# Memory values of a decoder trunk as seven half-size products, woven with two query heads (one core, Trainium2)

## The chip, the cores and the metric

The kernel runs on one core of one Trainium2 chip. The metric is the device time of one execution in microseconds (us). The kernel before took 1379.85 us in the median of three runs (1379.85 to 1380.17).

## The reference

Two decoder layers over x of 512 rows and 1024 columns. Each layer has three sub-layers, each `x = x + RMSNorm_post(f(RMSNorm_pre(x)))`: a mixer (layer 0: forgetting attention beside a gated convolution; layer 1: a recurrent block), a cross-attention of four heads into 256 memory rows, and a SwiGLU feed-forward of width 2816. The change is in the cross-attention:

```python
def memory_cross_attention(h, m, w_q, w_kv, w_o):
    q = (h @ w_q).reshape(bsz, seq, MEM_HEADS, MEM_HEAD_DIM)      # 4 heads of 256
    k, v = jnp.split(m @ w_kv, 2, axis=-1)                        # m: 256 x 1024
    s = jnp.einsum("bqhd,bkhd->bhqk", q, k) * (MEM_HEAD_DIM ** -0.5)
    p = jax.nn.softmax(s, axis=-1)
    o = jnp.einsum("bhqk,bkhd->bqhd", p, v).reshape(bsz, seq, D_MODEL)
    return o @ w_o
```

with `h = RMSNorm_pre(x)` and `m = RMSNorm(mem) * g_mem`. So the values are V = m @ W_v, a 256 x 1024 by 1024 x 1024 product in each layer.

## The kernel before

**Number format.** Every operand of a product is split into a high and a low part (`wh` and `wl`, `hTh` and `hTl`, `vh` and `vl`): ScalarE (ACT) casts the high part, VectorE (DVE) subtracts it from the source to get the low part. A product is three matmuls on TensorE (PE): high by high, high by low, low by high. A matmul here takes a 128 x 128 stationary operand and streams 512 columns. Weights come in pieces of 128 x 1024 values (512 KB) through a pool of four staging buffers `st`, and are split into pools of four `wh` and four `wl` buffers (`load_w`; `split_out` for other operands, L553-L562). Such a buffer can be cast into again when the last matmul that reads its old content is done.

**Order.** PE runs its instructions in the order of the program text. On ACT, DVE and GpSimd (POOL) a scheduler sets the order when the kernel is built; the chip then runs each engine's list from front to back, and an instruction that waits holds up all behind it on its engine. SyncE (SP) issues the weight loads and GpSimd some transfers.

**The stages around the change**, in each layer:
- The mixer's output projection (`OutProj.half1`, L613) goes over four blocks t of 128 rows. After each, `chain` (L637) ends the block: the square of the bank on ACT (`junk<-bB`, L221), the mean on DVE (`post`, L225 and L229), its power -0.5 on POOL (L233), the gain (`yb`, L642), and the two halves of the residual sum (`x`, L645). When block t has run half of its matmuls, `next` (L653) normalises block t-1 for the cross-attention: squares of x on ACT, `pre` on DVE (L225, L229) and POOL (L233), and two halves `h` on DVE (L259). Block t-2 is transposed there: eight 128 x 128 transposes on PE (L306), then `hTh` on ACT (L315) and `hTl` on DVE (L316). The transposes of block t need both halves of `h`.
- `memory_T` (L1019) makes the memory, transposed and scaled by its gain, in high and low parts `mT` (L1043, L1044) from `mTr` (the normalised memory without the gain).
- `memory_kv` (L1057) makes the keys in four quarters, each with two weight pieces and two banks of 8 steps (a 512-column and a 256-column matmul, L1071 and L1072, per step); each bank ends in `ks` on ACT and DVE (L1074, L1075), each quarter in the split `kh`, `kl`. Then `rest` transposes the last two row blocks, and the values are made: for each half of the columns four weight pieces, each used by two banks of three matmuls per step (L1088 to L1090), 96 matmuls in all, and a split `vh`, `vl` per bank.
- `cross` (L1095) makes the four query heads (`q_head`, L1102, 48 matmuls each by way of `ws_steps`), scores, softmax and the attention outputs, the first two query heads right after the values.
- In the feed-forward, `DownProj` already works with seven half-size products; its sums of weights are made in DRAM by copies (the list `copies`, which `pace` hands to SP behind the weight loads) and by adds (the list `adds`, accumulating transfers of GpSimd, which `spend` hands out at set places).

## Time and profile before

| | |
|---|---|
| median of three runs | 1379.85 us (1379.85 to 1380.17) |
| the profiled execution | 1379.94 us, of which the span from the first to the last instruction is 1378.2 us |
| mean granted PE clock | 0.999 |
| busy share of the span | PE 99%, DVE 81%, ACT 53%, POOL 8% |
| moved by DMA | 233.34 MB |
| keys, layer 0 | from 227.08 us |
| values, layer 0 | from 251.35 us |

In a timeline a row gives the start (us from the span's start), the duration, the engine, the line, output and inputs by their names, how many instructions run on in the row, and in brackets how long the engine had idled before it and what ended that. In a group of instructions the row gives the count, the busy time with the mean of one in ns, and the idle time ahead of them. Lines are those of the kernel before.

### The profile page before, as it was taken

How to read it: one execution, taken by the hardware profiler on the slowest of the kernel's cores; microseconds unless marked ns; L12 is line 12 of the kernel's file. 1: busy time of each engine (PE TensorE's matmuls, PEld its weight loads, DVE VectorE, ACT ScalarE, POOL GpSimd, SP SyncE). 2: the span in 40 equal slices, each digit the busy share in tenths (PEclk: the TensorE clock that was granted, in tenths of full speed). 3: DMA queues.
4: the chain of work that ended last, by engine and by line, in shares of the span. 5: the costliest groups of instructions: out<-in, count | busy, mean ns of one | idle time of the engine just before them, and what ended most of it. 6: DMA issues, size and time to landing. Idle time of an engine off the chain costs nothing.

```text
span 1378.2 us, 21545 instructions
## 1 busy us (share of the span) xinstructions
PE 1368.9 (99%) x8262; PEld 1217.7 (88%) x8262; DVE 1119.8 (81%) x1850; ACT 730.9 (53%) x1206; POOL 111.2 (8%) x160
## 2 busy tenths in 40 slices
PE   9999999999999999999999999999999999999998
PEld 7888788888899999998889888888889999999886
DVE  6777778635589999989898898764568999999987
ACT  5345466534464444456684896553456444445664
POOL 1000001012000101000011000101200011000001
PEclk9999999999999999999999999999999999999999
DMA  6854353668125557566666657357712555666654
GB/s 222 287 174 162 109 194 88 206 154 169 62 92 167 150 148 187 161 246 217 201 221 189 217 170 246 84 185 156 155 61 93 169 155 171 157 176 237 201 190 144
DMA packets 155107, 233.34 MB, mean 169 GB/s; under 512 B 8462, under 2 KB 90482, under 8 KB 153724
## 3 DMA queue, kind: packets, MB, share of 16 engines
q1 hardware_dynamic: 134420, 179.73, 39.5%
q0 software_dynamic: 17072, 46.16, 15.2%
q10 hardware_dynamic: 3512, 6.08, 1.4%
q8 instruction: 65, 1.06, 0.3%
q14 instruction: 38, 0.31, 0.1%
HBM read 219.34 MB, written 58.74 MB: 202 GB/s over the span
## 4 chain that ended last, share of the span: by engine, by line
PE 99%; DVE 0%; DMA 0%; ACT 0%; issue 0%; DVEq 0%; SPq 0%; ACTq 0%
PE bA L337 13%; PE bA L339 13%; PE bA L338 13%; PE bB L337 6%; PE bB L338 6%; PE bB L339 6%; PE bB L822 3%; PE bB L823 3%; PE bB L821 3%; PE bA L1071 2%; PE bA L822 2%; PE bA L823 2%; PE bA L821 2%; PE bA L580 2%; PE bA L582 2%; PE bB L582 2%
## 5 line engine op out<-in xcount | busy, mean ns | idle before, releaser
L557 DVE TENSOR_TENSOR wl<-st,wh 128x1024 fp32r<-128x1024 f32 x108 | 131.2, 1220 | 83.9 <-ACT wh L556 83.3
L556 ACT CAST wh<-st 128x1024 fp32r<-128x1024 f32 x108 | 113.1, 1050 | 107.9 <-PE bA L338 55.1
L337 PE MATMUL bA<-hTh,wh 128*128 128x512 f32 (+1 forms) x440 | 168.6, 383 | 0.0
L339 PE MATMUL bA<-hTh,wl 128*128 128x512 f32 (+1 forms) x440 | 165.6, 376 | 0.0
L338 PE MATMUL bA<-hTl,wh 128*128 128x512 f32 (+1 forms) x440 | 165.5, 376 | 0.0
L448 ACT CAST wg<-wr 128x1024 fp32r<-128x1024 f32 x80 | 83.6, 1046 | 48.9 <-DVE wr L477 38.5
L787 ACT CAST wh<-st 128x1024 fp32r<-128x1024 f32 x76 | 74.9, 985 | 62.4 <-PE bA L823 27.0
L449 DVE TENSOR_TENSOR wg<-wr,wg 128x1024 fp32r<-128x1024 f32 x80 | 97.1, 1214 | 0.0
L337 PEld LDWEIGHTS bA<-hTh,wh 128*128 128x128 f32 x440 | 82.9, 188 | 15.3 <-issue 1.0
L339 PEld LDWEIGHTS bA<-hTh,wl 128*128 128x128 f32 x440 | 82.8, 188 | 15.3
L338 PEld LDWEIGHTS bA<-hTl,wh 128*128 128x128 f32 x440 | 83.0, 189 | 13.8
L792 DVE TENSOR_TENSOR wl<-st,wh 128x1024 fp32r<-128x1024 f32 x76 | 86.1, 1133 | 10.2 <-ACT wh L787 10.1
L448 ACT CAST wh<-tt 128x1024 fp32r<-128x1024 f32 x40 | 42.1, 1053 | 61.4 <-DVE tt L477 61.4
L337 PE MATMUL bA<-hTq,wh 128*128 128x256 f32 x208 | 59.2, 284 | 0.0
L339 PE MATMUL bA<-hTq,wl 128*128 128x256 f32 x208 | 58.9, 283 | 0.0
L338 PE MATMUL bA<-hTq,wh 128*128 128x256 f32 x208 | 58.8, 283 | 0.0
L821 PE MATMUL bB<-wh,ya 128*128 128x512 f32 x148 | 57.6, 389 | 0.0
L822 PE MATMUL bB<-wl,ya 128*128 128x512 f32 x148 | 57.6, 389 | 0.0
L823 PE MATMUL bB<-wh,ya 128*128 128x512 f32 x148 | 57.6, 389 | 0.0
L767 DVE TENSOR_TENSOR ya<-yb,ya 128x512 fp32r<-128x512 f32 x84 | 53.3, 638 | 0.0
L821 PE MATMUL bA<-wh,ya 128*128 128x512 f32 x132 | 51.3, 389 | 0.0
L822 PE MATMUL bA<-wl,ya 128*128 128x512 f32 x132 | 51.3, 389 | 0.0
(385 smaller groups left out, 4396.9 us busy)
## 6 DMA issues: line engine op xcount, KB each, us to landing
wr<-in_w_ffn_gu_dram SPq DMA_DIRECT2D x80, 512.0 KB
st<-t SPq DMA_DIRECT2D x40, 512.0 KB
t<-in_w_ffn_down_dram SPq DMA_DIRECT2D x32, 512.0 KB
st<-in_w_xkv_dram SPq DMA_DIRECT2D x32, 512.0 KB
st<-in_w_ffn_down_dram SPq DMA_DIRECT2D x30, 512.0 KB
st<-in_ab_w_in_dram SPq DMA_DIRECT2D x24, 512.0 KB
y<-yr POOLq DMA_DIRECT2D x18, 512.0 KB, 4.7
t<-in_w_ffn_down_dram POOLq DMA_DIRECT2D x16, 512.0 KB, 8.7
```

What stands on the lines that cost most here:

```text
L337: nc.tensor.matmul(out=ps, lhsT=wh, rhs=xh, start=first, stop=False)
L338: nc.tensor.matmul(out=ps, lhsT=wh, rhs=xl, start=False, stop=False)
L339: nc.tensor.matmul(out=ps, lhsT=wl, rhs=xh, start=False, stop=last)
L448: return (lambda: nc.scalar.copy(out=to[0], in_=src), lambda: nc.vector.tensor_tensor(out=to[1], in0=src, in1=f(to[0]), op=ALU.subtract))
L449: lambda: nc.vector.tensor_tensor(out=to[1], in0=src, in1=f(to[0]), op=ALU.subtract))
L556: nc.scalar.copy(out=hi, in_=src)
L557: nc.vector.tensor_tensor(out=lo, in0=src, in1=f(hi), op=ALU.subtract)
L787: nc.scalar.copy(out=self.wt[s][0], in_=self.st[s])
L792: nc.vector.tensor_tensor(out=lo, in0=self.st[s], in1=f(hi), op=ALU.subtract)
L821: nc.tensor.matmul(out=banks[t], lhsT=yh, rhs=wh[:, jj, :], start=first and jj == 0, stop=False)
L822: nc.tensor.matmul(out=banks[t], lhsT=yh, rhs=wl[:, jj, :], start=False, stop=False)
L823: nc.tensor.matmul(out=banks[t], lhsT=yl, rhs=wh[:, jj, :], start=False, stop=last and jj == n - 1)
```

## The change

V in each layer, a product of a 2 x 2 by a 2 x 2 arrangement of blocks, is made with seven products of half the size in place of eight. With A = m in blocks a11, a12, a21, a22 (row blocks of 128 of the 256 memory rows by column blocks of 512) and B = W_v in blocks b11 to b22 (512 x 512), the products are, in this order, a11 b11, s2 t2, n3 t3, a22 t4, n1 t1, a12 b21, n4 b22, where the t are sums of weight blocks and the n and s2 sums of memory blocks. What it puts in:
- The four weight sums of a layer lie in DRAM. `plan` puts 8 copies (SP) and 8 accumulating adds (GpSimd) of 512 KB each into the lists; the adds of layer 0 are handed out inside the mixer (`early`), those of layer 1 with the ones of the feed-forward of layer 0.
- The four memory sums are made in place on `mTr` between the keys' quarters (`operands`): 8 multiplications of 128 x 256 on ACT, 4 subtractions of 128 x 512 on DVE, 4 splits `va` (ACT, DVE). They are issued behind the splits of quarters 0 and 1 and later.
- `begin` loads and splits the two pieces of b11 ahead of `rest`.
- `steps` makes the seven products; each of the 28 steps has 3 matmuls, and each product has two weight pieces of its own, so that there are 84 matmuls of 512 columns in place of 96 and 14 pieces in place of 8. The partial sums are carried in SBUF (`vp`, `vq`, `vv`, `vc`).
- In `cross`, `weave` runs these steps and those of query heads 0 and 1 by turns: 4 steps of the values first, then one of each. The query heads' pieces come into the same rotation of buffers.

The core of the diff:

```diff
+        def operands(self, raw, vhl, layer):
+            for k in range(KT):
+                nc.scalar.mul(out=raw[:, k, :], in_=raw[:, k, :], mul=ch("gm", 8 * layer + k))
+            yield
...
+            sub(a21, a21, a11)
+            sub(a22, a22, a21)
+            sub(a11, a11, a22)
+            sub(a12, a12, a22)
...
+        def begin(self):
+            self.ahead = [self.load("b11", k0) for k0 in (0, 2)]
...
+            for a_, b_ in self.ORDER:
+                ps = bankA() if b_ == "b11" else bankB()
+                for k0 in (0, 2):
+                    wh, wl = self.ahead.pop(0) if self.ahead else self.load(b_, k0)
+                    for kk in range(2):
+                        k = k0 + kk
+                        hi, lo = self.parts[a_][k]
+                        nc.tensor.matmul(out=ps, lhsT=hi, rhs=wh[:, kk, :], start=k == 0, stop=False)
+                        nc.tensor.matmul(out=ps, lhsT=hi, rhs=wl[:, kk, :], start=False, stop=False)
+                        nc.tensor.matmul(out=ps, lhsT=lo, rhs=wh[:, kk, :], start=False, stop=k == 3)
+                        yield 1
...
-            split_out(s, kh_[:, c, :], kl_[:, c, :])
+            last = split_out(s, kh_[:, c, :], kl_[:, c, :])
+            if values and c < 3:
+                if c == 0:
+                    operands = values.operands(raw, vhl, layer)
+                with tc.issue_after(last[0]), tc.issue_after(last[1]):
+                    next(operands, None)
+        if values:
+            values.begin()
         between()
...
+        if values:
+            weave(values.steps(), q_steps(0, 1, ahead=4))
+            vh, vl = values.out
+        else:
+            q_head(0)
+            q_head(1)
```

The rows below are engines' lists in the order in which they run, from the built programs; numbers behind a name tell buffers apart, and lines are those of the program that the row is from (those of the changed kernel lie one higher here: L317 is L316 of before).

The first place is DVE while PE is in the third and fourth row block of the mixer's output projection, layer 0. `x1` and `x2` are the second and third row block of the residual, `h` the normalised halves that the transposes read, `post_1931` and `post_1963` the mean square of the third row block's output. Before:

```order
L316 TENSOR_TENSOR hTl_1947<-bA_2129,hTh_1945 128x4x128 [waits Activation_49]
L316 TENSOR_TENSOR hTl_1948<-bA_2136,hTh_1946 128x4x128 [waits DMASW1_49,DVE_49,Activation_49]
L225 TENSOR_SCALAR pre_2143<-pre_2143 128x1 [waits Activation_49]
L229 SCALAR_TENSOR_TENSOR pre_2143<-pre_2143 128x1 [waits DVE_49,Activation_49]
L259 SCALAR_TENSOR_TENSOR h_2149<-x1_112,pre_2143,gain_1973 128x512 [waits Pool_49]
L259 SCALAR_TENSOR_TENSOR h_2151<-x1_112,pre_2143,gain_1975 128x512
L229 SCALAR_TENSOR_TENSOR post_1931<-post_1931 128x1 [waits Activation_49]
L642 TENSOR_TENSOR yb_2169<-bB_1979,gain_1753 128x512
L645 SCALAR_TENSOR_TENSOR x2_113<-ya_1940,post_1931,x2_113 128x512 [waits Pool_49]
L645 SCALAR_TENSOR_TENSOR x2_113<-yb_2169,post_1931,x2_113 128x512 [waits DVE_49]
```

The same place on DVE in the changed kernel:

```order
L317 TENSOR_TENSOR hTl_1979<-bA_2163,hTh_1977 128x4x128 [waits Activation_49]
L230 SCALAR_TENSOR_TENSOR post_1963<-post_1963 128x1 [waits Activation_49]
L646 SCALAR_TENSOR_TENSOR x2_113<-ya_1972,post_1963,x2_113 128x512 [waits Pool_49]
L317 TENSOR_TENSOR hTl_1980<-bA_2170,hTh_1978 128x4x128 [waits PE_49]
L226 TENSOR_SCALAR pre_2177<-pre_2177 128x1
L230 SCALAR_TENSOR_TENSOR pre_2177<-pre_2177 128x1 [waits DVE_49]
L260 SCALAR_TENSOR_TENSOR h_2183<-x1_112,pre_2177,gain_2005 128x512 [waits Pool_49]
L260 SCALAR_TENSOR_TENSOR h_2185<-x1_112,pre_2177,gain_2007 128x512
L643 TENSOR_TENSOR yb_2203<-bB_2011,gain_1785 128x512
```

What moved: `post` and the first half of the sum of `x2`, with its wait for POOL, stood behind the two `h` of `x1`; now they stand ahead of them, and ahead of the second `hTl` and of `pre`. Layer 1 has the same exchange at its output projection.

The second place is DVE from the end of the keys into the values, layer 0; `ks` and `kl` belong to the last keys, `hTl` to the four transposes of `rest`. Before, where the four `wl` are those of the first four values' pieces:

```order
L557 TENSOR_TENSOR wl_2489<-st_2486,wh_2488 128x1024
L557 TENSOR_TENSOR wl_2507<-st_2504,wh_2506 128x1024
L1075 TENSOR_TENSOR ks_2360<-bA_2380,ks_2360 128x256
L557 TENSOR_TENSOR kl_2241<-ks_2360,kh_2240 128x512
L1075 TENSOR_TENSOR ks_2413<-bA_2414,ks_2413 128x256
L557 TENSOR_TENSOR wl_2525<-st_2522,wh_2524 128x1024
L557 TENSOR_TENSOR wl_2543<-st_2540,wh_2542 128x1024
L1075 TENSOR_TENSOR ks_2413<-bA_2433,ks_2413 128x256
L316 TENSOR_TENSOR hTl_1947<-bB_2454,hTh_1945 128x4x128
L316 TENSOR_TENSOR hTl_1948<-bB_2461,hTh_1946 128x4x128
L557 TENSOR_TENSOR kl_2241<-ks_2413,kh_2240 128x512
```

The same place on DVE in the changed kernel, where `wl_2525` is the second piece of b11 (its first stands four rows ahead), `wl_2584` and `wl_2616` are the two pieces of t2, `wl_2593` and `wl_2599` those of query head 0, `wl_2636` the first of t3:

```order
L1173 TENSOR_TENSOR ks_2475<-bA_2495,ks_2475 128x256
L558 TENSOR_TENSOR wl_2525<-st_2522,wh_2524 128x1024
L558 TENSOR_TENSOR kl_2275<-ks_2475,kh_2274 128x512
L317 TENSOR_TENSOR hTl_1979<-bB_2528,hTh_1977 128x4x128
L317 TENSOR_TENSOR hTl_1980<-bB_2535,hTh_1978 128x4x128
L317 TENSOR_TENSOR hTl_1979<-bB_2542,hTh_1977 128x4x128
L317 TENSOR_TENSOR hTl_1980<-bB_2549,hTh_1978 128x4x128
L558 TENSOR_TENSOR wl_2584<-st_2581,wh_2583 128x1024
L558 TENSOR_TENSOR wl_2593<-st_2590,wh_2592 128x1024
L558 TENSOR_TENSOR wl_2599<-st_2596,wh_2598 128x1024
L558 TENSOR_TENSOR wl_2616<-st_2613,wh_2615 128x1024
L558 TENSOR_TENSOR wl_2636<-st_2633,wh_2635 128x1024
```

What moved: four pieces of the values were split ahead of the `hTl`; now two are, and the third (t2) stands behind the last `ks`, a `wl`, the `kl` and all four `hTl`, and the second piece of query head 0 stands ahead of the second of t2.

The third place is DVE near the end of the weave, layer 0, in the changed kernel alone: `wl_2774` and `wl_2780` are the pieces of query head 1, `wl_2797` is the second piece of b21, `vv`, `vq` and `vl` belong to the product with t1, `q` to query head 0:

```order
L558 TENSOR_TENSOR wl_2774<-st_2771,wh_2773 128x1024
L1062 TENSOR_TENSOR vv_2564<-bB_2710,vv_2564 128x512
L1062 TENSOR_TENSOR vq_2563<-bB_2710,vq_2563 128x512
L558 TENSOR_TENSOR wl_2780<-st_2777,wh_2779 128x1024
L558 TENSOR_TENSOR vl_2561<-vv_2564,vh_2560 128x512
L561 SCALAR_TENSOR_TENSOR q_2761<-bA_2603,q_2761 128x512
L558 TENSOR_TENSOR wl_2797<-st_2794,wh_2796 128x1024
```

What stands there now: the second piece of b21 is behind both pieces of query head 1 and the results of the product with t1. Its `wh_2796` is cast on ACT into the buffer that the second piece of query head 0 leaves, behind the cast for `wl_2780`, a `vh` and the second `q`.

More of the change, by code (lines that the diff above doesn't have):

```diff
@@ L1053, in memory_T, with memory_kv @@
         if layer:
-            return vhl, (lambda: parts(range(4)), lambda: parts(range(4, KT)))
-        return vhl, (lambda: turn(0), last)
-    def memory_kv(layer, vhl, between):
+            return (raw, vhl), (lambda: parts(range(4)), lambda: parts(range(4, KT)))
+        return (raw, vhl), (lambda: turn(0), last)
+    def memory_kv(layer, mem, between, values):
+        raw, vhl = mem
         w = a["w_xkv"][layer]
@@ L1093, in memory_kv, with cross @@
         return kh, kl, vh, vl
-    def cross(layer, hT, kv, proj, hTf):
+    def cross(layer, hT, kv, proj, hTf, values):
         kh, kl, vh, vl = kv
@@ L1100, in cross, with q_steps, put @@
         qs, ps_, pts = {}, {}, {}
-        def q_head(h):
-            banks = ws_gemm(wq, h * 256, hT)
-            q = group("q")
-            for m in range(2):
-                split_out(banks[m], q[:, m, :], q[:, 2 + m, :], scale)
-            qs[h] = q
-            spend(3, f(q)[:, 3, 511:512])
+        def q_steps(*hs, ahead=0):
+            yield ahead
+            for h in hs:
+                def put(banks, h=h):
+                    q = group("q")
+                    for m in range(2):
+                        split_out(banks[m], q[:, m, :], q[:, 2 + m, :], scale)
+                    qs[h] = q
+                    spend(3, f(q)[:, 3, 511:512])
+                yield from ws_steps(wq, h * 256, hT, put)
+        def q_head(h):
+            for _ in q_steps(h):
+                pass
         def scores(h):
@@ L1159, in av @@
                 o.hi[2 * h + m], o.lo[2 * h + m] = og[:, m, :], og[:, 2 + m, :]
-        q_head(0)
-        q_head(1)
+        if values:
+            weave(values.steps(), q_steps(0, 1, ahead=4))
+            vh, vl = values.out
+        else:
+            q_head(0)
+            q_head(1)
         scores(0)
@@ L1376, in fox, with early @@
         TO = [(0, 0), (1, 0), (2, 0), (1, 384)]
+        owed = [8 if 0 in SEVEN else 0]
+        def early(ap):
+            if owed[0]:
+                owed[0] -= 1
+                spend(1, ap)
         def y_group(m):
@@ L1626, in trunk_kernel @@
     hT = prev = None
+    values = {layer: Values(layer) for layer in SEVEN}
+    if 0 in values:
+        values[0].plan()
     for layer in range(2):
@@ L1638, in trunk_kernel @@
             rglru(hT, prev, pm)
-        vhl, steps = memory_T(layer, pm.first)
+        mem, steps = memory_T(layer, pm.first)
         pm.half1(steps)
@@ L1646, in rest @@
                 pm.transpose(t)
-        kv = memory_kv(layer, vhl, rest)
+        kv = memory_kv(layer, mem, rest, values.get(layer))
         hTf = new_quads()
         pc = OutProj(a["w_xo"][layer], None, KT, a["g_cross_post"][layer], a["g_ffn_pre"][layer], hTf)
-        cross(layer, hTc, kv, pc, hTf)
+        cross(layer, hTc, kv, pc, hTf, values.get(layer))
         hT = new_hT() if layer == 0 else None
         pf.hT = hT
+        if layer == 0 and 1 in values:
+            values[1].plan()
         ffn(layer, hTf, pc, pf)
```

72 lines of the change are left out of this document (69 added, 3 removed).

## The prediction

> **What bounds the kernel now.** I read the page first: which engine is busy, and of what the chain of work that ended last is made.
>
> ```profile
> PE 1368.9 (99%) x8262; PEld 1217.7 (88%) x8262; DVE 1119.8 (81%) x1850; ACT 730.9 (53%) x1206; POOL 111.2 (8%) x160
> ...
> PE 99%; DVE 0%; DMA 0%; ACT 0%; issue 0%; DVEq 0%; SPq 0%; ACTq 0%
> ```
>
> PE is the bound and nothing else is on the path. So a matmul that goes is worth its spacing, and a wait that PE is given is paid in full; the two add up. The windows show the stages around the change in layer 0: the keys (225 to 249), the values (249 to 272), query heads 0 and 1 (272 to 294), and the start of the span. The columns are the busy us and counts of PE, its weight loads, DVE, ACT and POOL, then the granted clock, the DMA share and GB/s.
>
> ```profile
> 0.00:2.00 2.00, 0.53 (x3) 0.53 (x4) 0.92 (x3) 0.63 (x1) 1.13 (x9) 1.00 0.16 29
> 2.00:4.00 2.00, 2.00 (x11) 2.00 (x10) 0.17 (x1) 0.86 (x2) 0.00 (x0) 1.00 1.04 273
> ...
> 225.00:249.00 24.00, 24.00 (x135) 20.72 (x134) 18.64 (x31) 14.00 (x28) 2.85 (x4) 1.00 0.55 149
> 249.00:272.00 23.00, 23.00 (x113) 19.38 (x112) 14.77 (x17) 12.68 (x17) 0.00 (x0) 1.00 0.57 182
> 272.00:294.00 22.00, 22.00 (x99) 18.22 (x98) 9.25 (x10) 6.97 (x9) 1.34 (x2) 1.00 0.54 146
> ```
>
> PE is full in all three stages. DVE comes next: the keys load it most (18.64 of 24), the values and query heads leave it 8 and 13 us free. So the amount of work on DVE does not decide; what decides is whether each low part is there when PE comes to it, and that hangs on its place in DVE's list, which runs front to back. For that I read PE's timeline at the two places where the changed list differs most: the last two row blocks of the mixer's projection, and the start of the values.
>
> ```profile
> 220.50 0.39 PE L582 MATMUL bB<-rh,y 128*128 128x512 f32 x1
> ...
> 223.46 1.03 PE L306 MATMUL bA<-ident,h 128*128 128x128 f32 x8
> 224.25 0.48 PE L580 MATMUL bB<-rh,y 128*128 128x512 f32 x1
> ...
> 249.68 1.91 PE L306 MATMUL bB<-ident,h 128*128 128x128 f32 x16
> 251.35 0.48 PE L1088 MATMUL bA<-wh,mT 128*128 128x512 f32 x1
> ...
> 273.20 0.39 PE L337 MATMUL bA<-hTh,wh 128*128 128x512 f32 x1
> ```
>
> The third row block's bank ends at 220.50 + 0.39 = 220.89; the transposes of the second start at 223.46 and the next matmul at 224.25, so eight transposes take 0.79. The keys' last matmul precedes 249.68; the values run from 251.35 to 273.20.
>
> **What goes: 24 matmuls.** The 96 matmuls of the values take 273.20 - 251.35 = 21.85 us, 0.228 each. 96 become 84 in each layer, of the same size: 24 × 0.228 = 5.5 us off the path. The query heads' 96 keep their number.
>
> **What is added off the path.** The durations are in the groups by line and shape.
>
> ```profile
> L557 DVE TENSOR_TENSOR wl<-st,wh 128x1024 fp32r<-128x1024 f32 x108 | 131.2, 1220 | 83.9 <-ACT wh L556 83.3
> L767 DVE TENSOR_TENSOR ya<-yb,ya 128x512 fp32r<-128x512 f32 x84 | 53.3, 638 | 0.0
> L557 DVE TENSOR_TENSOR vl<-bA,vh 128x512 fp32r<-128x512 f32 x8 | 5.5, 692 | 1.3 <-ACT vh L556 1.3
> L560 DVE SCALAR_TENSOR_TENSOR q<-bA,q 128x512 fp32r<-128x512 f32 x16 | 11.0, 687 | 10.0 <-ACT q L559 10.0
> L556 ACT CAST wh<-st 128x1024 fp32r<-128x1024 f32 x108 | 113.1, 1050 | 107.9 <-PE bA L338 55.1 <-issue 17.4 <-PE bA L1090 15.7
> L1043 ACT ACTIVATE mT<-mTr,chan 128x256 fp32r<-128x256 f32 x16 | 6.7, 503 | 0.9 <-DMA mTr<-memT 0.9
> L559 ACT ACTIVATE q<-bA 128x512 fp32r<-128x512 f32 x16 | 9.5, 594 | 15.0 <-PE bA L339 15.0
> ```
>
> Six more pieces in a layer cost 6 × 1.05 = 6.3 us on ACT and 6 × 1.22 = 7.3 on DVE, the combining steps on DVE about 7 × 0.65 = 4.6 (the nearest row is 0.638); the stages from 249 to 294 leave 25 us of ACT and 21 of DVE idle for that. As far as amounts go, it is hidden. The 16 copies (SP) and 16 adds (POOL) of 512 KB lie outside the weave, in the mixer and the feed-forward. POOL, 8% busy, had waited this long in the mixer of layer 0 before its next power was wanted:
>
> ```profile
> 205.35 0.56 POOL L233 TENSOR_TENSOR mem<-mem,nhalf 128x1 f32<-128x1 f32 x1 [52.72 <-DVE mem L229]
> ```
>
> I cost them at nothing; a rival says what late pieces cost.
>
> **What is moved, and PE's new waits.** There are four in a layer. Each is worked out as the time at which the changed list has DVE's result, less the time at which PE of before wants it.
>
> *First, the mixer's projection.* The rows of before for the chain of the third row block, and for the normalising of the second:
>
> ```profile
> 219.79 1.28 DVE L316 TENSOR_TENSOR hTl<-bA,hTh 128x512 fp32r<-128x512 f32 x2
> 220.99 0.14 DVE L225 TENSOR_SCALAR pre<-pre 128x1 f32<-128x1 f32 x1
> ...
> 222.09 1.41 DVE L259 SCALAR_TENSOR_TENSOR h<-x,pre,gain 128x512 f32<-128x512 f32 x2 [0.69 <-POOL pre L233]
> 223.42 0.15 DVE L229 SCALAR_TENSOR_TENSOR post<-post 128x1 f32<-128x1 f32 x1
> ...
> 224.23 0.75 DVE L645 SCALAR_TENSOR_TENSOR x<-ya,post,x 128x512 f32<-128x512 f32 x1
> 224.90 0.74 DVE L645 SCALAR_TENSOR_TENSOR x<-yb,post,x 128x512 f32<-128x512 f32 x1
> ```
>
> ```profile
> 221.48 0.20 ACT L221 ACTIVATION_READ_ACCUMULATOR junk<-bB 128x1 f32 x1
> ```
>
> Before, the first `h` is done at 222.84 and the second at 223.50, just as PE reaches them; there is nothing to spare. Now `post` and half of the residual sum of the third row block stand ahead. `post` can't start until ACT has that bank's square: 221.48 + 0.20 = 221.68, and 0.07 to hand it on. From `post` through POOL to the sum takes 224.23 - 223.42 = 0.81, the sum 0.67, the second `hTl` 0.64, from `pre` through POOL to `h` 222.09 - 220.99 = 1.10, the first `h` 0.75 (the second ends 0.66 later): 221.75 + 0.81 + 0.67 + 0.64 + 1.10 = 224.97, the second `h` is there at 226.38, and its four transposes are done at about 226.8, against 224.25: **2.6 us**. Queued behind the waiting `post` are both `h` and with them PE's transposes. The bank's end comes from PE and ACT's square from that bank, so nothing makes this earlier. Layer 1 has the same exchange, with PE's transposes at
>
> ```profile
> 875.06 1.03 PE L306 MATMUL bB<-ident,h 128*128 128x128 f32 x8
> ```
>
> ```profile
> 873.09 0.19 ACT L221 ACTIVATION_READ_ACCUMULATOR junk<-bA 128x1 f32 x1
> ```
>
> 873.28 + 0.07 + the same 4.63 + 0.40 = 878.4 against 875.06 + 0.79 = 875.85: 2.5. Bounds 2.2 to 3.0.
>
> *Second, the keys.* ACT gets 8 × 0.503 = 4.0 us of multiplications ahead of the third bank's `ks`, DVE 4 subtractions and 4 splits, 8 × 0.65 = 5.2 us. DVE was busy for 18.64 of 24; it is full now, and the low part of the last piece stands behind two of the subtractions. Bounds 0 and 0.8 (a subtraction and the hand-over); I take **0.4**.
>
> *Third, the head of the values.* The rows are those of DVE and ACT around 251:
>
> ```profile
> 250.90 1.23 DVE L557 TENSOR_TENSOR wl<-st,wh 128x1024 fp32r<-128x1024 f32 x1 [0.20 <-ACT wh L556]
> 252.04 0.42 DVE L1075 TENSOR_TENSOR ks<-bA,ks 128x256 f32<-128x256 f32 x1
> 252.38 1.28 DVE L316 TENSOR_TENSOR hTl<-bB,hTh 128x512 fp32r<-128x512 f32 x2
> ```
>
> ```profile
> 250.77 0.36 ACT L1074 COPY ks<-bA 128x256 f32<-128x256 f32 x1
> 251.03 2.05 ACT L315 CAST hTh<-bB 128x512 fp32r<-128x512 f32 x4
> ```
>
> The last `ks` can't be on DVE before ACT's, 251.13; then come, by the changed list, `ks` 0.42, the second piece of b11 1.2, `kl` 0.65, four `hTl` of 0.64 (1.28 for two) and the first of t2 1.2: 257.1. PE wants that at the 14th matmul, 251.35 + 13 × 0.228 = 254.3: 2.8 us. Before, four of the values' pieces were done by then, and the fifth was wanted at the 49th matmul. The query head's first piece comes 1.2 later and is wanted 3 matmuls later: 0.5 more. The second of t2 is behind the query head's second (2.4 us against 9 matmuls, 2.05): 0.4 more. Together 3.7 with DVE in time at the `ks`; with the keys' backlog another half us. I take **3.9**, bounds 3.2 and 4.6.
>
> *Fourth, the second piece of b21.* Its buffer is free when the 108th matmul has read the query head's second piece, and it is wanted 13 matmuls (3.0 us) later. DVE can't make the two sums before t1's last matmul, the 105th, is done; from there it has the hand-over 0.2, the sums 2 × 0.65, a `wl` 1.2, `vl` 0.69, `q` 0.69 and the piece's own `wl` 1.2, together 5.3 us. The low part is wanted 16 matmuls later, 3.6: 1.7 us late, less what the end of the query head leaves. I take **1.5**, bounds 0.8 and 2.
>
> Elsewhere in the weave a buffer has 16 matmuls, 3.6 us, from release to need, against 1.05 + 1.22 for its split: nothing.
>
> **The sum**: 2 × (0.4 + 3.9 + 1.5) + 2.6 + 2.5 = 16.7 us of waits, less 5.5, is +11.2. It is made against the profiled execution's 1379.94 us (0.09 above the median): **1391.1 us**, with bounds of 2 × (2.2 + 0 + 3.2 + 0.8) - 5.5 = +6.9 and 2 × (3.0 + 0.8 + 4.6 + 2) - 5.5 = +15.3: 1387 to 1395.
>
> **The rivals.**
>
> *Faster: the waits are hidden.* If every low part is in time, PE runs 5.5 us less: 1374.5. For it speaks the idle DVE in the stages; it decides as long as the waits of a layer stay below 2.73 us. Against it: the exchange in the projection alone, with no slack before it, comes to 2.5. I give it 0.06, and 0.03 to a close on either side of no change.
>
> *The exchange in the projection costs nothing,* say because PE's transposes are themselves behind something I don't see: 1391.1 - 5.1 = 1386.0. The rows speak against it. 0.12.
>
> *Late pieces.* The weave takes one and a half pieces in 12 matmuls, 0.786 MB in 2.72 us, 289 GB/s, where the row of the values has 182 at a share of 0.57, so some 320 when full. If the pieces come only at 182 GB/s, the 18 pieces (9.44 MB) of a layer need 51.9 us against 180 matmuls' 41.0: 10.9, of which 5.4 are counted: 2 × 5.5 more, 1402. 0.07.
>
> *A slower PE after the waits.* If the clock fell after the four waits over 2 us and PE ran at half its rate for some 3.7 us after each, 4 × 1.85 = 7.4 more: 1398.5. The rows show 1.5 us idle at the start, and a granted clock of 1.00 after it; a longer idle time is nowhere. 0.04. The Trainium skill's TensorE: Matmul & The Clock Gate, section HAM oscillation — how this bites in real kernels, warns of PE idle gaps above about 3.4 us; my longest single wait, 2.8, lies below that, so by this rule nothing is lost, and the trace agrees as far as its 1.5 us goes.
>
> **How the numbers follow.** The forecast as summed has 0.68: 1391.1. For the range I go down to 1384, which takes in the rival at 1386.0 with its own uncertainty, and up to 1399, which takes in the slower clock; left out are the faster cases and the late pieces, 0.16. A measurement of this kernel can tell about 0.2% (2.8 us) from no change. Faster 0.06, same 0.03, slower 0.91.
>
> **What would show it.** In the changed profile: PE idle for 2.5 us ahead of the transposes in the third and fourth row block of each projection, released by DVE's `h` (L260); ahead of the second matmul of t2, 2 us or more released by `wl` (L558); about 1.5 us at the second piece of b21; PE's other spacings as before. A PE without waits, or waits that `st` and its transfers end, would make the sum wrong, as would a granted clock below 0.99.

## The result, and the profile after

The changed kernel takes 1392.43 us in the median of five runs (1391.74 to 1394.37), the kernel before 1380.10 in five runs beside it (1379.85 to 1380.26). The ratio is 1.0094, with a 95% interval of 1.0082 to 1.0105: slower by 12.3 us. The forecast was 1391.1, with a range of 1384 to 1399. The profiled execution took 1394.00 us, 14.06 above that of before (1379.94); what follows is made against that pair.

The page of the changed kernel, its first part and its chain:

```profile
PE 1371.4 (99%) x8238; PEld 1216.8 (87%) x8238; DVE 1152.4 (83%) x1892; ACT 753.4 (54%) x1244; POOL 134.3 (10%) x184
...
PE 94%; DVE 4%; ACT 1%; issue 0%; DMA 0%; POOL 0%; DVEq 0%; SPq 0%; ACTq 0%; POOLq 0%
```

There are 24 matmuls fewer, and yet PE is busy for 2.5 us longer: its matmuls have become slower somewhere. DVE has come onto the path, with 4%. The view of PE's waits says where (in all, times, longest; in us):

```profile
PE bB L1077 <- DVE wl L558: 7.1, 4, 2.4
PE bB L307 <- DVE h L260: 2.4, 2, 2.1
PE bA L307 <- DVE h L260: 2.3, 1, 2.3
```

These are the places of the forecast: the transposes of the mixer's projection (L307), and low parts of the values' pieces (L1077). In PE's timeline of layer 0 the last bracket of a row is the idle time ahead of it:

```profile
222.47 0.39 PE L582 MATMUL bB<-rl,y 128*128 128x512 f32 x1
...
225.40 1.29 PE L307 MATMUL bA<-ident,h 128*128 128x128 f32 x8 [2.32 <-DVE h L260]
226.44 0.50 PE L581 MATMUL bB<-rh,y 128*128 128x512 f32 x1
...
230.64 0.39 PE L583 MATMUL bB<-rh,y 128*128 128x512 f32 x1
...
260.65 0.61 PE L1077 MATMUL bB<-wl,va 128*128 128x512 f32 x1 [2.30 <-DVE wl L558]
...
264.40 0.40 PE L339 MATMUL bA<-hTl,wh 128*128 128x512 f32 x1
...
288.24 0.50 PE L1077 MATMUL bB<-wl,mT 128*128 128x512 f32 x1 [1.21 <-DVE wl L558]
```

And in layer 1:

```profile
884.10 1.32 PE L307 MATMUL bB<-ident,h 128*128 128x128 f32 x8 [2.06 <-DVE h L260]
...
919.39 0.58 PE L1077 MATMUL bB<-wl,va 128*128 128x512 f32 x1 [2.37 <-DVE wl L558]
...
947.01 0.50 PE L1077 MATMUL bB<-wl,mT 128*128 128x512 f32 x1 [1.21 <-DVE wl L558]
```

Six waits, 11.47 us together. They don't cover +14.06 plus the 5.5 us of the matmuls that went. The rest is in the spacing of PE's matmuls behind the waits. From 226.44 to 230.64 are 12 matmuls, 11 spacings, 4.20 us; at the 0.228 of before they would be 2.51. The windows of 2 us around the first wait (PE, its weight loads, DVE, ACT, POOL with counts, the granted clock, DMA share, GB/s):

```profile
224.00:226.00 2.00, 0.60 (x4) 0.42 (x4) 1.50 (x3) 0.00 (x0) 0.47 (x1) 1.00 0.00 0
226.00:228.00 2.00, 1.96 (x9) 1.66 (x9) 1.83 (x4) 1.79 (x4) 0.00 (x0) 0.69 0.03 8
228.00:230.00 2.00, 2.00 (x6) 1.59 (x5) 1.15 (x5) 0.72 (x2) 0.55 (x1) 0.50 0.00 0
230.00:232.00 2.00, 2.00 (x11) 1.64 (x11) 1.27 (x4) 0.69 (x2) 0.00 (x0) 0.96 0.00 0
```

PE is idle for 2.32 us up to 225.40; the clock is still 1.00 when it starts again, and 0.50 from 226.8 on: six to nine instructions run where eleven do in the last row. It lasts for some 3.4 us. The same follows each of the four waits over 2 us: 1.69 and 1.68 us lost in the matmuls behind the transposes, 1.70 and 1.70 behind t2 (260.65 to 264.40 is 3.75 for 9 spacings, 2.05 at full clock). That is 6.8. None follows the waits of 1.21. The eight transposes themselves take 1.04 and 1.07 in place of 0.79, but not from the clock, which is still full there: the fifth waits for the second half of `h` (DVE ends it at 225.92, the transpose starts at 226.06 in layer 0): 0.25 and 0.28, 0.5 in all.

The sum of the profile: 11.47 idle, 0.5 between the transposes, 6.8 at half clock, and 6 × 0.16 = 1.0 because the matmul ahead of a wait is counted to its end (0.39) and not to the next one's start (0.228), less 5.5 for 24 matmuls, is +14.3; measured +14.06. The other four executions granted a mean clock of 0.993 to 0.998 where the profiled one had 0.993. A mean of 0.997 or 0.998 leaves room for at most two slow stretches in place of four, and yet these three executions are only 1.6 to 2.3 us shorter than the profiled one: in the whole time a slow stretch costs less than its 1.7 us (the two edits together, below, show the same).

### The profile page after: what moved, and what is told of

Same layout as the page of the kernel before. It is cut to its first block, busy times and chain, and to the rows that moved or that the text cites. A ratio compares the mean times of both kernels' runs of the same rounds, so it can differ in the third digit from the quotient of the medians.

```text
span 1391.9 us, 21677 instructions
## 1 busy us (share of the span) xinstructions
PE 1371.4 (99%) x8238; PEld 1216.8 (87%) x8238; DVE 1152.4 (83%) x1892; ACT 753.4 (54%) x1244; POOL 134.3 (10%) x184
## 4 chain that ended last, share of the span: by engine, by line
PE 94%; DVE 4%; ACT 1%; issue 0%; DMA 0%; POOL 0%; DVEq 0%; SPq 0%; ACTq 0%; POOLq 0%
PE bA L338 13%; PE bA L340 13%; PE bA L339 13%; PE bB L338 6%; PE bB L339 6%; PE bB L340 6%; PE bB L823 3%; PE bB L824 3%; PE bB L822 3%; PE bA L823 2%; PE bA L824 2%; PE bA L822 2%; PE bB L582 2%; PE bB L581 2%; PE bB L583 2%; PE bA L583 2%
## 5 line engine op out<-in xcount | busy, mean ns | idle before, releaser
L558 DVE TENSOR_TENSOR wl<-st,wh 128x1024 fp32r<-128x1024 f32 x120 | 145.2, 1219 | 55.5 <-ACT wh L557 55.0
L557 ACT CAST wh<-st 128x1024 fp32r<-128x1024 f32 x120 | 125.3, 1051 | 110.8 <-PE bA L339 36.2
L788 ACT CAST wh<-st 128x1024 fp32r<-128x1024 f32 x76 | 74.9, 986 | 64.0 <-PE bA L824 27.0
L793 DVE TENSOR_TENSOR wl<-st,wh 128x1024 fp32r<-128x1024 f32 x76 | 86.1, 1132 | 9.9 <-ACT wh L788 9.9
L234 POOL TENSOR_TENSOR post<-post,nhalf 128x1 f32<-128x1 f32 x23 | 14.3, 620 | 440.1 <-DVE post L230 426.6
```

The lines of the kernel that those rows point to most:

```text
L557: return (nc.scalar.copy(out=hi, in_=src).ins, nc.vector.tensor_tensor(out=lo, in0=src, in1=f(hi), op=ALU.subtract).ins)
L558: nc.vector.tensor_tensor(out=lo, in0=src, in1=f(hi), op=ALU.subtract).ins)
L788: nc.scalar.copy(out=self.wt[s][0], in_=self.st[s])
L793: nc.vector.tensor_tensor(out=lo, in0=self.st[s], in1=f(hi), op=ALU.subtract)
```

## The experiments

Two questions were open. The first is what makes the six waits. For the transposes: the *list* (`post` and the sum of x stand ahead of the normalising, as the forecast had it) or a *buffer*. In the rows of the order on record the second `hTl` of the first row block waited, before, for a transfer, DVE and ACT, and now for PE. `mTr` lives on in the changed kernel, since the memory sums are made in it in place. The `hTl` that took its buffer has to take another, `rl`, the low part of the projection's last weights, which PE reads in layer 0 until the 11th matmul of the fourth row block; in layer 1 the buffer comes free with the 6th. And `next` issues `h` of the second row block behind that `hTl`, by an edge. For the head of the values: the *amount* of work on DVE ahead of t2, or its place in the *list*. The second question is the *clock*: whether it is the idle time alone that halves it. Each run has its own runs of the kernel before beside it, with a median of 1379.70 for the list alone, the untied `h`, the pieces one at a time and the subtractions on GpSimd, of 1380.03 for the memory loaded a second time and the rest of the change, and of 1379.48 for the other four. Gains are given as the difference of the losses: the changed kernel was 12.3 above the runs beside it. Edits are to the changed kernel where nothing else is said.

### The list alone undone

`post` is issued behind the last `h`, in the order of before; the buffer stays as it is.

```diff
         def chain(self, t, ps):
...
-            r = rstd(st)
+            with tc.issue_after(last_h[0]) if self.behind_h and t else nullcontext():
+                r = rstd(st)
```

> The list at the mixer's projection is put back as it was before the change: both halves of h of the second row block stand ahead of post and the residual sum of the third, by an edge from h to post; nothing else is edited (the scheduler also turns some rows of the keys around). Theory 'list' (the prediction's step): PE's wait at the transposes in the fourth row block, 2.32 us in layer 0 and 2.06 in layer 1, is gone. Rival 'buffer': the memory's mTr now lives on into the keys, so the second low half hTl takes the buffer of the first tail weights' low part, which PE reads until the 12th matmul of the fourth row block; h stands behind that hTl by an edge of its own. Then the wait stays at 2.0 to 2.5 us in both layers whatever post does, and the time stays within 4 us of the changed kernel's 1392.4.

One run: 1397.39 us. DVE's timeline and PE's, layer 0 but for the last row, which is from layer 1 (this kernel's lines lie up to four higher; L586 is the product with `rl`):

```profile
223.09 0.69 DVE L319 TENSOR_TENSOR hTl<-bA,hTh 128x512 fp32r<-128x512 f32 x1 [3.03 <-PE bB L586]
```

```profile
225.69 1.29 PE L309 MATMUL bA<-ident,h 128*128 128x128 f32 x8 [2.49 <-DVE h L262]
...
227.05 0.39 PE L586 MATMUL bB<-rl,y 128*128 128x512 f32 x1
227.28 0.39 PE L587 MATMUL bB<-rh,y 128*128 128x512 f32 x1
...
884.87 1.32 PE L309 MATMUL bB<-ident,h 128*128 128x128 f32 x8 [1.30 <-DVE h L262]
```

DVE now stands idle for 3.03 us at the second `hTl` until PE has done with `rl`, and PE's wait at the transposes of layer 0 is as long as ever, 2.49: there the *buffer* alone is enough for it. In layer 1 (the last row) the wait falls from 2.06 to 1.30, where 2.0 to 2.5 was expected: there the buffer alone costs 1.30, and the *list* the other 0.76. The run has a wait that is not part of the question, 8.6 us in the keys (`wl` for L1175, two times 4.3): the edge gave the scheduler another list there. So its time, 5.0 above the changed kernel's where within 4 was expected, says nothing on the transposes. The two rows of 227.05 and 227.28 show something else: behind 2.49 us of idle time the matmuls are 0.23 apart, at full clock.

### `h` untied

The edge from the transposes of t-2 to `h` of t-1 is left out for t = 2.

```diff
-                        self.next(t - 1, self.transpose(t - 2, self.first) if t > 1 else ())
+                        turned = self.transpose(t - 2, self.first) if t > 1 else ()
+                        self.next(t - 1, turned if t != self.loose else ())
```

> The edge that ties h of the second row block behind the transposes and hTl of the first is taken out; the buffers are as in the changed kernel. Theory 'buffer': h no longer stands behind the hTl that waits for PE, and PE's wait at those transposes goes in both layers: 2 x 2.2 to 2.5 us of wait, and with it 2 x 1.9 us in which PE ran at half its clock behind the wait; some of it can come back in the keys, whose work on DVE is then nearer to PE: 1384 to 1388 us. Theory 'list': the same wait goes, 1384 to 1388 as well; what tells the two apart is the run before this one. Rival 'PE must wait there anyhow': 1391 to 1393.

Four runs: 1387.51 us (1387.37 to 1388.17), ratio to before 1.0055 (1.0039 to 1.0072): 7.8 above before, 4.5 less than the changed kernel's 12.3. DVE's timeline in layer 0:

```profile
221.41 1.41 DVE L260 SCALAR_TENSOR_TENSOR h<-x,pre,gain 128x512 f32<-128x512 f32 x2 [0.69 <-POOL pre L234]
222.74 0.15 DVE L230 SCALAR_TENSOR_TENSOR post<-post 128x1 f32<-128x1 f32 x1
...
224.23 0.68 DVE L317 TENSOR_TENSOR hTl<-bA,hTh 128x512 fp32r<-128x512 f32 x1
```

The transposes' waits are gone in both layers; the `hTl` that waits for `rl` runs behind `h`, where it holds up nobody. `post` stands behind `h` again without any edge that says so. The waits at the values are as in the changed kernel; the longest new one, 0.9 at L1173, is in the keys of one layer.

### The memory loaded a second time

The other side of the same cause: `mTr` is given up where it was before, and the sums are made in a second copy that is loaded from DRAM (one 1 MB load more in a layer).

```diff
                 if c == 0:
-                    operands = values.operands(raw, vhl, layer)
+                    again = f(group("mTr")).rearrange("p a (b c) -> p (a b) c", c=MEM)
+                    nc.sync.dma_start(out=again, in_=memT)
+                    operands = values.operands(again, vhl, layer)
```

> The changed kernel, but the memory operands are made from a copy of the memory that is loaded anew from DRAM when the keys begin, so that mTr ends where it ended before the change; the list keeps post ahead of h. Theory 'buffer': the second hTl gets mTr's buffer again and no longer waits for PE; h then has only post in front of it. If the buffer alone made the wait, PE's 2.32 and 2.06 us at the transposes of the fourth row block shrink to under 0.5 us. Rival 'list': they stay. The load of 1 MB stands in SP's queue among the keys' weights and the multiplications wait for it on ACT, so new waits of some us before or in the values are expected in either case, and the time says little.

One run: 1394.08 us. DVE's timeline, PE's, and PE's longest wait:

```profile
219.22 1.28 DVE L317 TENSOR_TENSOR hTl<-bA,hTh 128x512 fp32r<-128x512 f32 x2
...
221.51 1.41 DVE L260 SCALAR_TENSOR_TENSOR h<-x,pre,gain 128x512 f32<-128x512 f32 x2 [0.69 <-POOL pre L234]
222.84 0.15 DVE L230 SCALAR_TENSOR_TENSOR post<-post 128x1 f32<-128x1 f32 x1
```

```profile
222.88 1.03 PE L307 MATMUL bA<-ident,h 128*128 128x128 f32 x8
```

```profile
PE bA L1077 <- DVE wl L558: 6.0, 4, 3.1
```

Both `hTl` run together as they did before, the transposes of the fourth row block wait for nothing in either layer, and the order of before is back by itself. So the buffer is the cause, and the order on which the forecast was built is its consequence. Which of the two ends the wait differs by layer. In layer 0 of the changed kernel the sum of x ends at 222.77 and the buffer comes free at 222.86, 0.09 later: either alone would have cost about as much. In layer 1 the matmul that frees the buffer (the 6th of the fourth row block, which the run with the list undone shows as the releaser) ends at 880.68, and the second `hTl` starts a good 0.9 later, straight behind the sum of x:

```profile
880.95 0.75 DVE L646 SCALAR_TENSOR_TENSOR x<-ya,post,x 128x512 f32<-128x512 f32 x1 [0.66 <-POOL post L234]
881.62 0.68 DVE L317 TENSOR_TENSOR hTl<-bB,hTh 128x512 fp32r<-128x512 f32 x1
```

There it is the order that PE's wait hangs on, as forecast. An order changed without the buffer never stood in a run. The 1 MB more and the pieces behind it bring waits of their own in the values, L1077, so the time is no better.

### Query-head pieces split one at a time

`ws_steps` of the first query head splits its second piece where it is needed, not together with the first.

```diff
-            wh, wl = ws[kh]
+            wh, wl = load_w(w, 4 * kh, 4, c0, 256) if lazy else ws[kh]
```

> In the weave each query head loads and splits its second weight piece only when it comes to it, not both at its start. Theory: the wait at the second piece of b21 (1.21 us in each layer) is from the pieces of query head 1 that stand ahead of it on ACT and DVE and from the buffer of query head 0's second piece; it goes in both layers, 2.4 to 3 us less than the changed kernel: 1389 to 1390.5. The wait at t2 (2.3) stays. Rival 'late transfers': 18 pieces in the weave come too slowly; then the wait stays, at this piece or another, and the time is within 1 us of the changed kernel.

Four runs: 1388.08 us (1386.44 to 1388.52), ratio 1.0058 (1.0043 to 1.0073): 8.4 above before, 3.9 less than the changed kernel's 12.3. PE's waits at the values, and the window behind the one at t2 in layer 0:

```profile
PE bB L1077 <- DVE wl L558: 4.6, 2, 2.3
```

```profile
261.00:263.00 2.00, 2.00 (x8) 1.39 (x9) 2.00 (x2) 0.53 (x1) 0.00 (x0) 1.00 0.43 145
```

The two waits of 1.21 at the second piece of b21 are gone, 2 × (1.21 + 0.16) = 2.7 us. The two at t2 stay, but here the same wait of 2.3 us was followed by a granted clock of 1.00. From the end of that wait to the start of the 20th matmul behind it PE took 4.94 us here and 6.26 in the changed kernel, 1.3 less, and as much in layer 1. So the profiled executions, 1394.00 and 1388.52, differ by 2.7 + 2 × 1.3 = 5.3 of 5.5. That the 1.2 us left between the medians are clock too fits mean clocks of 0.996 to 0.999, but is not shown.

### The two together

Both edits.

> The edits of the second and the third run together: h untied from the first row block's transposes, and each query head's pieces loaded one at a time. They took 4.9 and 4.35 us off the changed kernel's 1392.4. Theory 'separate waits': they act at different places and add up: 1382.5 to 1384; left are the wait at t2 (2.3 to 2.4 in both layers, with half clock behind most of them) and about 0.9 in the keys of layer 0. Rival 'one chain': a wait that goes makes the next one longer, as with the subtractions on GpSimd; then 1386 to 1388.

Seven runs: 1383.65 us (1382.48 to 1384.72), ratio 1.0026 (1.0015 to 1.0037): 4.2 above before, 8.2 less than the changed kernel's 12.3, where the parts give 4.5 + 3.9 = 8.4. Of the six waits two are left:

```profile
PE bB L1080 <- DVE wl L558: 4.7, 2, 2.4
```

In the profiled execution, the slowest of the seven (1384.72, mean clock 0.997), both are followed by half clock; the two executions with a mean of 0.999, which leaves room for no such stretch, took 1382.48 and 1382.82. So here two slow stretches are worth about 2 us of the whole time.

### Four pieces ahead

The head of the values by its list: the two pieces of t2 are loaded and split together with those of b11, ahead of `rest`, where before had four pieces too.

```diff
-            self.ahead = [self.load("b11", k0) for k0 in (0, 2)]
+            self.ahead = [self.load(n, k0) for n, k0 in (("b11", 0), ("b11", 2), ("t2", 0), ("t2", 2))]
```

> The changed kernel with both pieces of t2 loaded and split along with those of b11, so that their low parts stand ahead of the four hTl in DVE's list. Theory 'list': the wait at the second matmul of t2, 2.30 and 2.37 us, goes and no other takes its place: 1384 to 1386. Theory 'amount': between the last ks and the first query head's matmuls DVE has the same work in another order; t2 is in time, but the hTl come 2.4 us later, and the first matmul that needs them or their bank waits 2 to 3.5 us in sum: 1391 to 1394.

One run: 1394.80 us, 0.8 above what the theory of the amount expected. PE's waits, and DVE's timeline in layer 0:

```profile
PE bB L1076 <- DVE hTl L317: 4.1, 2, 2.0
...
PE bA L340 <- DVE wl L558: 1.7, 2, 1.2
```

```profile
255.90 2.35 DVE L558 TENSOR_TENSOR wl<-st,wh 128x1024 fp32r<-128x1024 f32 x2
258.17 2.47 DVE L317 TENSOR_TENSOR hTl<-bB,hTh 128x512 fp32r<-128x512 f32 x4
```

t2 is in time; now PE waits 2.0 in each layer for the `hTl` that stand behind it, and then for the query head's piece. DVE has no idle time there in either order. So at this place the *amount* decides, and a new order only chooses who waits.

### The subtractions on GpSimd

The four subtractions of memory blocks go from DVE to GpSimd.

```diff
-            sub = lambda o, i0, i1: nc.vector.tensor_tensor(out=o, in0=i0, in1=i1, op=ALU.subtract)
+            sub = lambda o, i0, i1: nc.gpsimd.tensor_tensor(out=o, in0=i0, in1=i1, op=ALU.subtract)
```

> The four subtractions of the memory operands (128 x 512, 0.65 us each on DVE) go to GpSimd. Theory 'amount': DVE is full from the keys on, so that what stands ahead of t2's wl is late by as much as the keys' work on DVE was increased; with 2.4 to 2.7 us taken off, PE's wait at the second matmul of t2 (2.30 and 2.37 us) and the half clock behind it (1.7 us each) go: 1384 to 1386. Rival 'list': t2's wl stands behind ks, kl and four hTl, which depend on PE and ACT and not on how much DVE did before; the wait stays at 2 us or more and the time at 1390 to 1393. Rival 'slow GpSimd': its subtractions take so long that the splits va come late and PE waits for them.

Four runs: 1392.32 us (1391.77 to 1392.53), ratio 1.0090 (1.0075 to 1.0105): no change. PE's waits, and POOL's and DVE's timelines in layer 0:

```profile
PE bA L1170 <- DVE wl L558: 4.1, 2, 2.4
PE bB L1077 <- DVE wl L558: 3.5, 4, 1.2
```

```profile
241.29 1.29 POOL L1034 TENSOR_TENSOR mTr<-mTr 128x512 f32<-128x512 f32 x1 [4.47 <-ACT mTr L1030]
242.95 5.44 POOL L1034 TENSOR_TENSOR mTr<-mTr 128x512 f32<-128x512 f32 x3 [0.37 <-ACT mTr L1030]
```

```profile
245.46 1.78 DVE L558 TENSOR_TENSOR kl<-ks,kh 128x512 fp32r<-128x512 f32 x1
247.16 2.39 DVE L558 TENSOR_TENSOR va<-mTr,va 128x512 fp32r<-128x512 f32 x2
```

The wait at t2 falls from 2.3 to 0.5, and new ones stand in the keys (L1170), 4.1 in two. So the time is the one that the theory of the list expected, but not for its reason: with less work on DVE ahead of it t2 did come earlier, and the loss passed to the keys. GpSimd's subtraction takes 1.29 alone, three take 5.44; and of the DVE rows that run in that time `kl` takes 1.78 and the two `va` 2.39, where `kl` of the changed kernel takes 0.68 and its two `va` 1.28. So DVE loses 2.2 us in place of 4 × 0.65 = 2.6. The Trainium skill, SBUF — State Buffer, section SBUF: two separate sides, says that a GpSimd operation that reads SBUF and a DVE operation with two SBUF inputs lock each other out of a shared pair of ports, each for a whole instruction; the trace agrees with that: `kl` and the first `va`, which start while a GpSimd subtraction runs, lose 1.1 us each, while the `wl` that starts 0.01 us ahead of one (244.31) takes its usual 1.22, and that GpSimd subtraction 2.37 in place of 1.29.

### The operands behind the keys

Untied `h`, pieces one at a time, and the four memory sums and their splits issued behind the keys and not between their quarters. The product a12 b21, that needs none of them, comes second, so that t2 is wanted later.

```diff
-        ORDER = (("a11", "b11"), ("s2", "t2"), ("n3", "t3"), ("a22", "t4"), ("n1", "t1"), ("a12", "b21"), ("n4", "b22"))
+        ORDER = (("a11", "b11"), ("a12", "b21"), ("s2", "t2"), ("n3", "t3"), ("a22", "t4"), ("n1", "t1"), ("n4", "b22"))
...
-            if values and c < 3:
-                if c == 0:
-                    operands = values.operands(raw, vhl, layer)
-                with tc.issue_after(last[0]), tc.issue_after(last[1]):
-                    next(operands, None)
...
         between()
         if values:
+            for _ in values.operands(raw, vhl, layer):
+                pass
```

> As the run before, and in addition the memory operands (8 multiplications, 4 subtractions, 4 splits) are made behind the keys and their transposes and not between the quarters, and the product a12 b21, which needs none of them, comes second (its sum with a11 b11 goes into a buffer of its own). Theory 'amount': the keys then load DVE and ACT as before the change; the waits in the keys and at the second product's low part go, 2 x 2.4 + 0.9, and the half clock behind them, 2 x 1.7: 1374 to 1377, faster than the kernel before (1379.7). Rival 'list': the second product's first piece still stands behind ks, kl and four hTl; its wait of 2.3 stays and the time is 1381 to 1384. Rival 'moved on': the operands' 5.2 us on DVE and 6.3 on ACT in the weave make waits there: 1378 or more.

Five runs: 1375.00 us (1374.39 to 1375.34), ratio 0.9966 (0.9953 to 0.9978): 4.5 us faster than before, 16.8 better than the changed kernel's +12.3, and 8.7 of that from this last step. PE's longest wait behind the span's start, and the windows of the values and the query heads in layer 0:

```profile
PE bA L1389 <- ACT wh L1414: 0.5, 1, 0.5
```

```profile
249.00:272.00 23.00, 22.71 (x110) 18.81 (x109) 19.31 (x23) 15.36 (x21) 0.00 (x0) 1.00 0.70 237
272.00:294.00 22.00, 22.00 (x105) 18.46 (x104) 16.61 (x20) 12.16 (x15) 4.47 (x4) 1.00 0.89 245
```

PE is full again but for 0.29 us at an `hTl`, at a clock of 1.00 throughout. DVE has the same work as in the changed kernel, but 16.61 of 22 us of it in the query heads' window, where before had 9.25. The first piece of the second product still stands behind the last `ks`, the `kl` and the `hTl` in DVE's list, and PE does not wait for it: its place in the list does not make it late. So the matmuls that went are worth nearly the 5.5 us of the forecast once nothing waits.

### Idle time by measure

The kernel before, with `wl` of some of the values' pieces written several times over: four places, two in each layer. Nothing else is changed and the output is the same.

```diff
                 st = load_raw(w, k2, 2, D + nh * 512, 512)
                 wh, wl = split_w(st, 2, 512)
+                for _ in range({(0, 1, 2): 4, (0, 1, 6): 4, (1, 1, 2): 4, (1, 1, 6): 5}.get((layer, nh, k2), 0)):
+                    nc.vector.tensor_tensor(out=wl, in0=st, in1=f(wh), op=ALU.subtract)
```

> The kernel before; at two pieces of the values in each layer the low part is written again 4, 4, 4 and 5 times by DVE, the same numbers each time, so that PE has to wait for it: by the rows' 1.2 us each about 2.5 and 1.5 us in layer 0 and 2.5 and 3.7 in layer 1. Theory 'clock': behind an idle time of 2 us or more PE runs at half its clock for 3 to 3.5 us (8 matmuls at 0.427 in place of 0.228), behind 1.5 it doesn't; the sum is 1379.7 + 10.2 + 2 or 3 x 1.7 = 1393 to 1395. Rival 'waits alone': the clock stays and the sum is 1379.7 + 10.2 = 1390.

One run: 1393.52 us, 14.0 above before. PE's wait for these rewrites, and the windows behind the first, of 2.31 us ahead of 267.18:

```profile
PE bA L1092 <- DVE wl L1085: 8.0, 3, 3.3
```

```profile
268.00:270.00 2.00, 2.00 (x7) 1.60 (x6) 2.00 (x3) 0.00 (x0) 0.00 (x0) 0.63 0.85 257
270.00:272.00 2.00, 2.00 (x6) 1.54 (x5) 1.75 (x2) 0.79 (x1) 0.00 (x0) 0.52 0.62 187
```

One of the four places gave no wait. The three that did are 8.0 us of idle time (2.31, 2.31, 3.35); the other 6.0 of the 14.0 are at most 2.0 for each: the hand-over takes 0.16 of that, and a wait near the start that is 0.4 longer than before as much again, which leaves 1.7. All three were followed by half clock, in a kernel that has nothing of the change in it. So idle time is enough to halve the clock.

### The rest of the change

The values of both layers by the eight products of before, everything else as in the changed program.

```diff
-SEVEN = 0, 1
+SEVEN = ()
```

> The changed kernel's program with the seven products switched off in both layers: the values are made as before, and what is left of the change is the new rule by which the feed-forward hands out its adds. Theory: that rule costs nothing, 1379.3 to 1380.3 us. Rival: part of the loss is in the feed-forward's adds; then more than 1381.

Ten runs: 1379.43 us (1379.10 to 1380.75), ratio 0.9997 (0.9988 to 1.0007). What the diff changes besides costs nothing; the whole +12.3 belongs to the seven products and what is made for them.

## Why the prediction was right, and where not

The direction, the places and the time were right: 1391.1 forecast, 1392.43 measured. That it came so close is in part luck. PE's waits, with the hand-over and the wait for the second `h`, came to 11.5 + 1.0 + 0.5 = 13.0 us where the sum had 16.7; against that stands the half clock, 6.8 in the profiled execution, which the sum put at nothing.

**The matmuls that go.** 5.5 us was right: the version without waits gained 4.5 of it in measured time, with 0.5 us of a wait at 12.8 us, far ahead of the change, that before had not (the run of the rest of the change has 0.7 there).

**The projection.** Forecast 2.6 and 2.5 for the delay of the product behind the transposes. Measured are 2.32 and 2.06 of idle time, and with the hand-over and the wait for the second `h` 2.7 and 2.5: the size is right. So is the chain that the forecast describes ("Queued behind the waiting `post` are both `h`"): in layer 1 PE's wait hangs on it (the buffer by itself would have made 1.30). The step that failed is its cause: the forecast took the place of `post` in the list for the origin of the wait, and left the buffer out. DVE's timeline of the changed kernel in layer 0 shows both chains:

```profile
221.18 0.16 DVE L230 SCALAR_TENSOR_TENSOR post<-post 128x1 f32<-128x1 f32 x1 [1.24 <-ACT junk L222]
222.02 0.75 DVE L646 SCALAR_TENSOR_TENSOR x<-ya,post,x 128x512 f32<-128x512 f32 x1 [0.69 <-POOL post L234]
222.89 0.69 DVE L317 TENSOR_TENSOR hTl<-bA,hTh 128x512 fp32r<-128x512 f32 x1
```

`post` came 0.6 us earlier than forecast, as PE was 0.5 earlier in that execution, and the sum of x ended at 222.77. `hTl` could not start before the end of PE's last product with `rl` ahead of the wait, 222.47 + 0.39 = 222.86. With the list turned back, the wait stayed in layer 0 and lost 0.76 in layer 1; with the buffer given back, it went in both, and the order with it. The forecast read the names in the rows of the order, but not what its own row said of the second `hTl`: it waits for PE. An instruction of a transposed block that waits for PE is odd, and asking which PE instruction it waits for would have led to the buffer.

**The keys.** Forecast 0.4 in a layer, measured none. The full DVE delayed what comes next, not the keys.

**The head of the values.** Forecast 3.9 in three waits (2.8, 0.5, 0.4, and 0.2 for the keys' backlog), measured one of 2.30 and 2.37, at the second matmul of t2 as forecast:

```profile
256.99 2.47 DVE L317 TENSOR_TENSOR hTl<-bB,hTh 128x512 fp32r<-128x512 f32 x4
259.39 4.61 DVE L558 TENSOR_TENSOR wl<-st,wh 128x1024 fp32r<-128x1024 f32 x4
```

The first of these four `wl` is t2's, behind the `hTl`, without a gap in DVE's work from 244.49 on. The 0.5 was too large: the query head's low part is wanted four matmuls behind t2's, not three, and at full clock (the pieces one at a time) it was about 0.1 late. The 0.4 did not come in the profiled execution, since PE ran at half clock: 12 matmuls of 0.228 behind 260.65 would have been at 263.39, and the low part of t2's second piece was done at 264.00. That it would have come at full clock is an estimate from these rows, not shown. Wait and slow PE together are 2.3 + 1.7 = 4.0, the size of the sum; how it is made up was wrong. That the amount decides, and not the place in the list as the prediction had it ("the amount of work on DVE does not decide"), is the second step that failed: with t2 put forward the wait passed to `hTl` and the query head, and only moving work to a later stage removed it.

**The second piece of b21.** Forecast 1.5, bounds 0.8 to 2, measured 1.21 in both layers.

**The slower PE.** This rival had 0.04 and a price of 4 × 1.85 = 7.4, of four waits over 2 us. It happened as described, in four places, with 6.8 in the profiled execution; the 3.7 us of its price stand in no row of before, and a slow stretch measured 3.4. The time did not come to its 1398.5 because the waits were 3.7 us shorter than the sum (13.0 in place of 16.7) and half clock costs the whole time less than it costs the matmuls behind the wait. It was put low by a row of 1.5 us of idle time with a clock of 1.00 behind it, and by a page. That row was misread. PE's timeline of before has the same transposes behind it and 7 us later:

```profile
1.47 3.03 PE L1257 MATMUL bA<-ident 128*128 128x128 f32 x13 [1.47 <-POOL ident masks.py:199]
...
8.33 0.60 PE L1257 MATMUL bA<-ident 128*128 128x128 f32 x4
```

They are 0.21 us apart in the first row and 0.11 in the second, so PE ran at half rate there; the trace's record of the clock begins only at 5.76. What PE did ahead of the span is in no trace, so the row speaks neither for nor against the rival. The forecast's own sign, a mean clock below 0.99, was too coarse: four slow stretches bring it to 0.993. The rows behind the waits show that 2.06 us are enough. The Trainium skill, TensorE: Matmul & The Clock Gate, section HAM oscillation — how this bites in real kernels, warns of idle gaps above about 3.4 us; here the trace does not agree, the measurement decides. The Trainium skill, on the same page, section What's actually happening, has a window of about 3.4 us that runs free of the kernel; with that agree the length of the slow stretches, 3.41 us, that they start whole multiples of it apart (226.76 and 260.89 in the changed kernel are ten of them apart), and that the same wait has it in one run and not in another.

**Late pieces** did not occur: no wait of PE in the values is ended by `st`.

## What to carry to other kernels

A tile that is kept alive longer costs where its buffer would have gone next, possibly in another stage: when an instruction's list of waits changes, find out which buffer it has inherited and who still reads that. Work that is hidden by the average can stand in the one stage that is full; there an order only chooses who waits, and moving the work to the next stage (here behind the keys), with the other two edits, turned +12.3 us into -4.5. And a wait of PE of about 2 us or more can cost 1 to 1.7 us beyond its length.

## What the runs showed of the hardware

**Half clock after 2 us of idle time.** Over all profiles of this case, PE's idle waits of 2.03 to 2.49 us were followed by a granted clock of 0.50 for about 3.4 us (6.8 in one) in 17 of 24 cases, those of 3.14 to 4.34 us in 4 of 4, those of 1.2 to 1.64 in 1 of 16, and that one shares its slow stretch with a wait of 2.03 shortly ahead of it. Whether it comes after 2.0 to 2.5 us is not set by the length: 2.06 had it, 2.49 had not.

What sets it can be read from the same traces. In each of the nine that have slow stretches between start and end, these begin on a grid of 3.413 us. Cut along it, a stretch at full clock was followed by a slow one in 21 of the 22 cases in which PE was idle for 1.68 us or more of it (the exception had 1.74), and in none in which it was idle for 1.67 or less. Of the 2.06 us in layer 1 of the changed kernel 1.98 fell into one stretch; the 2.06 us at the same place with the subtractions on GpSimd were split into 0.47 and 1.59, the 2.49 with the list undone into 1.64 and 0.85, and these two had no slow stretch. The grid does not begin with the kernel (the first edge on record lies between 4.62 and 7.60 us), so the same wait can fall either way from run to run; no run shifted a wait on purpose. With that fits how the runs scatter (2.6 us among five runs of the changed kernel, 0.4 among the five of before beside them, up to 1.5 in the larger sets).

In the matmuls behind the wait a case costs 1.7 us; against a restart at full clock 1.3 (6.26 in place of 4.94 us behind t2), and in the whole time about 1 (two stretches, 2 us, in the two edits together).

**GpSimd beside DVE.** A GpSimd subtraction of 128x512 took 1.29 us alone. Beside three of them two DVE subtractions of that size lost 1.1 us each; a `wl` that started just ahead of one lost nothing, and the GpSimd subtraction took 2.37.
